# Bias rows by copies on GpSimd, index weights turned through DRAM, and two small sample blocks moved behind the value bundles

## The chip, the core and the metric

The kernel runs on one core of one Trainium2 chip. The metric is device time in microseconds (us) of one launch, and the profile is one execution of the same program.

## What is computed

One step of a hybrid layer for two requests that share every weight: a prompt of 256 frames and a sample of 32 new frames of a running stream (T = 288 rows of width 1024 together). One input projection gives everything. Branch A is an mLSTM (4 heads of 256, gates, state). Branch B is sparse attention (8 heads of 128). In it an indexer with 8 heads of 64 scores the keys,

```
score[t, s] = sum_h w[t, h] * relu(q_idx[t, h] . k_idx[s])     # w scaled by constants
keep the 64 best (prompt) or 72 best (sample) keys of a row
logits = q . k * 128**-0.5 + rel_bias[bucket(s - t)]           # 32 buckets, 8 heads
```

and the kept keys are attended to. Both branches go through gates and output weights, then a residual and a layer norm. All of it is float32; products of large size are made in two parts (a high and a low part of each operand, three matmuls).

## The kernel before

**Tiles and slots.** The weights are cut into 117 tiles of 128x1024, in the order of `ORDER`: the small columns (`sm`: index key, gates, index weights), index queries, `qb`/`kb` of branch B, its values `vb`, then `qa`/`ka`/`va`, gates, and the output weights. One tile is one slot. In each slot the tile is multiplied with x (24 matmuls of 288 columns, lines 896 to 898). In the value slots (`vb`, `va`, eight each) x stands still and the weights stream (lines 912 to 914). The sample's 32 rows are done behind every fourth value tile, in a block of 32 matmuls that each fill one strip of 32 output rows (line 920). I call this block the value bundle's strip block.

**What sets the order.** It is written out: `side()` runs in the middle of each slot's matmuls. It first runs jobs set for that slot by `at`, then one step of each generator in `procs`; a `yield` ends a step. Engines keep program order. Weight tiles come by `load_tile` on SyncE's queue (line 121), nine slots ahead, into 8 buffers. ScalarE makes the high part (line 132), VectorE the low part (line 139). A value tile's buffer is free only when the strip block has read it.

**The bias table** (`bias_table`, from slot 8). A one-hot matrix of 576 columns and the 32x8 `rel_bias` give an 8x576 table by four matmuls in slot 9, copied to SBUF by ScalarE. Two slots on SyncE writes rows of it to DRAM (line 218) and reads them back shifted as the bias `bm` and `bms`.

**The index weights** (`index_weights`, started in slot 7). They are rows 68 to 75 of the small tile `sm`. Three transposes on the matrix engine (lines 279, 280) turn them; VectorE scales them into `wn` and `wp0` and copies `ws` together (lines 282 to 288). `index()` uses them from slot 8 on, the sample's `ws` in slot 11.

**The sample's logits** (`attn_sample`, line 496) are 32 matmuls into strips of 32 rows, in the slot in which `bm` has been masked, four slots behind the last `vb` tile. VectorE and ScalarE then do the softmax (lines 502 to 506). **The sample's mLSTM scores** (`mlstm_sample`, line 718) are 16 recorded matmuls of 32x32 in slot `zb` 2, behind the transposes of attention head 7 (line 568).

**Banks.** Matmul results lie in two banks for the slots' products (`proj`) and six for all else (`bank`); a value bundle holds three of the six.

Of the kernel before, what the change touches and what calls it, by code (L numbers as in the profile page):

```python
# [10 lines left out]
F32 = mybir.dt.float32  # L11
# [23 lines left out]
ALPHA = 2.0 ** 0.25  # L35
LN_EPS = 1e-5
HEAD_EPS = 1e-6
NREL = 576
REL0 = 287
MASK = -1e30  # L40
NOT_ADMISSIBLE = -3.0e38
TAKEN = -3.39e38
# [43 lines left out]
def body(ctx, tc, a, o):  # L86
# [10 lines left out]
    def bank(name, n=512):  # L97
        return ps.tile([128, 512], F32, name=name, tag="side", bufs=6)
# [56 lines left out]
    bms = early[:, 512:1088].rearrange("p (g t) -> p g t", g=2)  # L155
    kiT = early[:, 1088:1376]
    cki = early[:, 1376:1632]
    early2 = sb("early2", [128, 2 * NREL], tag="vaT")
    oneh = early2[:32, 0:NREL]
    rtab = early2[:8, NREL:2 * NREL]  # L160
    lead = [sb(f"wst_k{k}", [128, KT * 128], tag="wst", bufs=8) for k in range(KT)]
    cut = T + 128
    sp.dma_start(lead[0][:, 0:cut], a["first"][:, 0, 0:cut])
# [21 lines left out]
    sp.dma_start(cst, a["cst"])  # L185
    load_tile(FIRST + 3)
    ident, smask, stack = cst[:, 0:128], cst[:, 128:160], cst[:, 160:288]
    relb = sb("relb", [32, 8])
    sp.dma_start(relb, a["rel_bias"])
    sp.dma_start(oneh, a["onehot"])  # L190
    load_tile(FIRST + 4)
    for c in range(2):
        sp.dma_start(cki[64 * c:64 * c + 64], a["cache_idx_k"])
# [3 lines left out]
    def bias_table():  # L197
        r = rtab
        row = dr.tile([8, 384], F32, name="rrow")
        rows = dr.tile([8, 320], F32, name="rrows")  # L200
        scr = dr.tile([128, 8, 384], F32, name="rscr")
        scs = dr.tile([TS, 8, 320], F32, name="rscs")
        early3 = sb("early3", [128, NREL + 256], F32R, tag="a5")
        onehr, rel = early3[:, :NREL], early3[:, NREL:]
        relh, rell = rel[:, 0:128], rel[:, 128:256]
        pool.memset(early3.bitcast(F32), 0.0)
        act.copy(onehr[:32], oneh)
        act.copy(relh[:32, :8], relb)
        dve.tensor_tensor(rell[:32, :8], relb, relh[:32, :8].bitcast(F32), OP.subtract)
        yield  # L210
        half = NREL // 2
        for c in (0, half):
            p = bank(f"rb{c}")
            pe.matmul(p[:, :half], lhsT=relh, rhs=onehr[:, c:c + half], start=True, stop=False)
            pe.matmul(p[:, :half], lhsT=rell, rhs=onehr[:, c:c + half], start=False, stop=True)
            act.copy(r[:, c:c + half], p[:8, :half])
        yield
        sp.dma_start(row, r[:, REL0 - 255:REL0 + 129])
        sp.dma_start(rows, r[:, 0:320])
        yield  # L220
        yield
        for c in range(0, 128, 64):
            sp.dma_start(scr[c:c + 64], ap_of(row, 0, [[0, 64], [1, 8 * 384]]))
            yield
        sp.dma_start(scs, ap_of(rows, 0, [[0, TS], [1, 8 * 320]]))
        yield
        yield
        yield
        bm = sb("bm", [128, 8, 384], tag="a5")
        store["bm"] = bm  # L230
        sp.dma_start(bm[:, :, 0:256], ap_of(scr, 127, [[8 * 384 - 1, 128], [384, 8], [1, 256]]))
        yield
        for i in range(4):
            sp.dma_start(bms[32 * i:32 * i + 32],
                         ap_of(scs, i * 320 + 31, [[8 * 320 - 1, TS], [4 * 320, 2], [1, T]]))
        yield
        yield
        pool.tensor_copy(bm[:, :, 256:384], bm[:, :, 128:256])
# [1 line left out]
    start(8, bias_table())  # L240


    wn = sb("wn", [128, 2, 8])
    wp0 = sb("wp0", [128, 4])
    ws = sb("ws", [128, 2])
    gnat = sb("gnat", [128, 2, 3, 4])
# [12 lines left out]
    def small_parts():  # L259
        sm = store["sm"]  # L260
        act.copy(kiT[0:64], sm[0:64])
        dve.tensor_copy(kiT[64:128], sm[0:64])
        act.copy(kih, kiT[:, :TP])
        dve.tensor_tensor(kil, kiT[:, :TP], kih.bitcast(F32), OP.subtract)
        gt = sb("gt", [4, 7, T], tag="stC")
        ig, z = gt[:, 0], gt[:, 1]
        store["gt"] = gt
        store["ig"], store["z"] = ig, z
        act.activation(ig, sm[64:68], AF.Identity, bias=small[:, 0:1])
        dve.tensor_scalar(z, sm[96:100], small[:, 1:2], None, op0=OP.add)  # L270
        start(cur[0] + 1, gates())
        start(cur[0] + 1, index_weights())
        at(cur[0] + 3, lambda: sp.dma_start(o["idx_k"], kiT[0:64]))

    def index_weights():
        sm = store["sm"]
        p = bank("wn_p")
        for b in range(2):
            pe.transpose(p[:, 128 * b:128 * b + 128], sm[:, 128 * b:128 * b + 128], ident)
        pe.transpose(p[:TS, 256:384], sm[:, TP:T], ident)  # L280
        c8 = float(np.float32(IH ** -0.5))
        dve.tensor_scalar(wn[:, 0], p[:, 128 + 68:128 + 76], c8, ID ** -0.5, op0=OP.mult, op1=OP.mult)
        dve.tensor_scalar(wn[:TS, 1], p[:TS, 256 + 68:256 + 76], c8, ID ** -0.5, op0=OP.mult, op1=OP.mult)
        for e in range(2):
            dve.tensor_scalar(wp0[64 * e:64 * e + 64], p[64:128, 68 + e:76:2], c8, ID ** -0.5, op0=OP.mult, op1=OP.mult)
        yield
        for i in range(4):
            dve.tensor_copy(ws[32 * i:32 * i + 32], wn[:TS, 1, 2 * i:2 * i + 2])

    def gates():  # L290
        ig, z = store["ig"], store["z"]
# [96 lines left out]
    def index():  # L388
# [3 lines left out]
        for j in range(IH // 2):  # L392
# [8 lines left out]
            for e in range(2):  # L401
                h = 2 * j + e
                n = 256 + 128 * e
                r = sb(f"r{h}", [128, 384], tag="lg", bufs=3)
                act.activation(r[:, :n], p[e][:, :n], AF.Relu)
                for c, w in ((slice(0, 256), wn[:, 0, h:h + 1]), (slice(256, 384), wp0[:, j:j + 1]))[:1 + e]:
                    if j == 0 and (e == 0 or c.start):
                        dve.tensor_scalar(acc[:, c], r[:, c], w, None, op0=OP.mult)
                    else:
                        dve.scalar_tensor_tensor(acc[:, c], r[:, c], w, acc[:, c], op0=OP.mult, op1=OP.add)  # L410
# [73 lines left out]
        pe.matmul(out, lhsT=lh, rhs=rl, start=False, stop=False)  # L484
        pe.matmul(out, lhsT=ll, rhs=rh, start=False, stop=last)

    def attn_sample():
        while "masked" not in store:
            yield
        two = range(2)  # L490
        q = [bank(f"as{g}") for g in two]
        for c, keys in ((slice(0, 256), lazy["ckT"]), (slice(256, T), kbT[:, :, TP:T])):
            for g in two:
                for i in range(4):
                    h = 4 * g + i
                    pe.matmul(q[g][32 * i:32 * i + 32, c], lhsT=qbT[:, h, TP:T], rhs=keys[:, h], start=True, stop=True)
        lgs = []
        for g in two:
            lg = sb(f"lgs{g}", [128, 384], tag="lg", bufs=3)[:, :T]
# [190 lines left out]
    def head_norm(h, num, emn, **kw):  # L690
# [18 lines left out]
            act.activation(hn[:, b], num[b][:, 0:256], AF.Identity, bias=dd[:, b, 0:1], scale=dd[:, b, 1:2])  # L709
        return hn  # L710

    def mlstm_sample():
        stC = lazy["stC"]
        q3 = qaT[:, :, TP:T]
        s = bank("ss")
        for h in range(AH):
            for kd in range(2):
                pe.matmul(s[32 * h:32 * h + 32, 0:TS], lhsT=kaT[:, 2 * h + kd, TP:T], rhs=q3[:, 2 * h + kd],
                          start=(kd == 0), stop=(kd == 1))
        tail = sb("tail", [128, 2, 4, TS], tag="ba", bufs=2)  # L720
        for kd in range(2):
            pool.tensor_copy(tail[:, kd], kaT[:, kd:8:2, TP:T])
# [178 lines left out]
    def values(t, n, k, side):  # L901
        if k == 0:
            b = [bank(f"{n}p{i}") for i in range(3)]
            lazy["vp"] = b[:2] + [out_bank(t) for _ in range(2)] + b[2:]
        banks = lazy["vp"]
        wh, wl = split.pop(t)
        for i in range(4):
            if i == 2:
                side()
            r = slice(128 * (i // 2), 128 * (i // 2) + 128)  # L910
            c = slice(512 * (i % 2), 512 * (i % 2) + 512)
            pe.matmul(banks[i], lhsT=xh[:, k, r], rhs=wh[:, c], start=(k == 0), stop=False)  # L912
            pe.matmul(banks[i], lhsT=xh[:, k, r], rhs=wl[:, c], start=False, stop=False)  # L913
            pe.matmul(banks[i], lhsT=xl[:, k, r], rhs=wh[:, c], start=False, stop=(k == KT - 1))  # L914
        if k % 4 == 3:
            for kk in range(k - 3, k + 1):
                g = 2 if n == "vb" else 1
                w = stage[t - k + kk].rearrange("p (g i c) -> p i g c", g=g, i=4)
                for i in range(4):
                    pe.matmul(banks[4][32 * i:32 * i + 32, 0:256].rearrange("p (g c) -> p g c", g=g),  # L920
                              lhsT=xs0[:, kk], rhs=w[:, i], start=(kk == 0), stop=(kk == KT - 1))
        return banks if k == KT - 1 else None

    def natural(t, rows, columns=(0, 1)):
        k = t - POS["wo", 0]
# [176 lines left out]
def constants():  # L1102
# [3 lines left out]
    s, l = np.meshgrid(i, i, indexing="ij")  # L1106
    cst[:, 128:160] = np.tile(np.where(s > l, MASK, 0.0)[:TS, :TS], (4, 1))
    cst[:, 160:288] = i[:, None] % 32 == i[None, :] % 32
    rel = np.arange(NREL) - REL0
    n = np.abs(rel)  # L1110
    bucket = np.where(n < 8, n, 8 + sum((n >= c).astype(np.int64) for c in (12, 16, 23, 32, 46, 64, 91)))
    bucket = bucket + np.where(rel > 0, 16, 0)
    onehot = np.zeros((32, NREL), np.float32)
    onehot[bucket, np.arange(NREL)] = 1.0
    return cst, onehot


def pack_weights(x, w_in, w_out_a, w_out_b, w_o):
# [76 lines left out]
```

## Time and profile before

| | |
|---|---|
| time, median of 3 runs | 428.74 us (428.34 to 429.11) |
| profiled execution, own time | 429.2 us |
| its span, first to last instruction | 427.1 us |
| granted TensorE clock | 0.999 of full speed |
| PE (matmul) busy | 420.4 us, 98% |
| VectorE (DVE) busy | 299.0 us, 70% |
| ScalarE (ACT) busy | 226.7 us, 53% |
| GpSimd (POOL) busy | 22.6 us, 5% |

Busy time counts an instruction from its start to its end; matmuls overlap, so a matmul of 0.29 us may start 0.13 us behind the one before. What a stretch costs is read from starts. In a timeline a row is start, duration, engine, line, operation, output <- inputs, shape and count (several of one kind are merged), and in brackets the idle time of its engine before it and what ended that. SPq rows are the issue of DMAs, not the transfers.

### The profile page before, as it was taken

The numbers are of one execution on the slowest core, as the hardware profiler recorded it, in microseconds if no ns is written. First come the engines' busy times: TensorE is split into PE (matmuls) and PEld (weight loads), VectorE is DVE, ScalarE is ACT, GpSimd is POOL, SyncE is SP. The second block draws the span as 40 slices with busy tenths as digits, with TensorE's granted clock in tenths as the row PEclk, the third lists the DMA queues.
The fourth block names the chain that finished last, engine by engine and source line by source line (L and its number), as shares of the span: only waits on it lengthen the run. The fifth ranks groups of instructions, "written<-read, shape, count | busy, mean of one in ns | idle before, by whom it ended". The sixth has DMA issues, their size and how long they took to land.

```text
span 427.1 us, 8153 instructions
## 1 busy us (share of the span) xinstructions
PE 420.4 (98%) x3189; PEld 395.6 (93%) x3189; DVE 299.0 (70%) x601; ACT 226.7 (53%) x443; POOL 22.6 (5%) x41
## 2 busy tenths in 40 slices
PE   8999999999999999999999999999999999999994
PEld 7999999878999998789999999999999999998874
DVE  5669989986756665665999987876454465665674
ACT  6776445425666666458795465555434444446402
POOL 0000000000400000000001101101000000000031
PEclk9999999999999999999999999999999999999999
DMA  8987869575945630349544456545555658543014
GB/s 305 362 319 206 294 204 309 214 198 204 411 156 147 218 122 0 114 141 335 152 148 150 109 171 215 148 148 151 168 178 155 176 163 265 153 137 124 27 46 140
DMA packets 29746, 78.81 MB, mean 185 GB/s; under 512 B 8548, under 2 KB 11852, under 8 KB 28908
## 3 DMA queue, kind: packets, MB, share of 16 engines
q1 hardware_dynamic: 28844, 76.98, 56.0%
q10 hardware_dynamic: 864, 1.32, 0.9%
q8 instruction: 25, 0.41, 0.4%
q14 instruction: 13, 0.11, 0.1%
HBM read 72.52 MB, written 7.67 MB: 188 GB/s over the span
## 4 chain that ended last, share of the span: by engine, by line
PE 96%; DVE 1%; ACT 1%; POOLq 0%; issue 0%; DVEq 0%; ACTq 0%
PE pj L896 22%; PE pj L897 22%; PE pj L898 21%; PE yn L938 5%; PE pj L957 3%; PE pj L912 2%; PE pj L914 2%; PE pj L913 2%; PE warm_p L150 1%; PE vap L912 1%; PE vbp L912 1%; PE vbp L914 1%; PE vap L920 1%; PE vbp L920 1%; PE vap L914 1%; PE vbp L913 1%
## 5 line engine op out<-in xcount | busy, mean ns | idle before, releaser
L132 ACT CAST wh<-wst 128x1024 fp32r<-128x1024 f32 x112 | 117.8, 1052 | 137.5 <-PE pj L897 64.8
L896 PE MATMUL pj<-xh,wh 128*128 128x288 f32 x576 | 171.7, 298 | 0.1
L897 PE MATMUL pj<-xl,wh 128*128 128x288 f32 x576 | 169.9, 295 | 0.0
L898 PE MATMUL pj<-xh,wl 128*128 128x288 f32 x576 | 169.8, 295 | 0.0
L139 DVE TENSOR_TENSOR wl<-wst,wh 128x1024 fp32r<-128x1024 f32 x112 | 136.3, 1219 | 32.2 <-ACT wh L132 31.9
L896 PEld LDWEIGHTS pj<-xh,wh 128*128 128x128 f32 x576 | 108.3, 188 | 1.8 <-issue 0.4
L897 PEld LDWEIGHTS pj<-xl,wh 128*128 128x128 f32 x576 | 108.3, 188 | 0.1
L898 PEld LDWEIGHTS pj<-xh,wl 128*128 128x128 f32 x576 | 108.3, 188 | 0.0
L896 PE MATMUL pj<-bbh,wh 128*128 128x288 f32 x64 | 18.9, 295 | 0.0
L897 PE MATMUL pj<-bal,wh 128*128 128x288 f32 x64 | 18.9, 295 | 0.0
L898 PE MATMUL pj<-bah,wl 128*128 128x288 f32 x64 | 18.9, 295 | 0.0
L897 PE MATMUL pj<-bbl,wh 128*128 128x288 f32 x64 | 18.9, 295 | 0.0
L898 PE MATMUL pj<-bbh,wl 128*128 128x288 f32 x64 | 18.8, 294 | 0.0
L896 PE MATMUL pj<-bah,wh 128*128 128x288 f32 x64 | 18.8, 293 | 0.0
L912 PE MATMUL pj<-wh,xh 128*128 128x512 f32 x32 | 13.0, 405 | 0.0
L938 PE MATMUL yn<-wh,mxh 128*128 128x512 f32 x32 | 12.9, 404 | 0.0
L938 PE MATMUL yn<-wl,mxh 128*128 128x512 f32 x32 | 12.7, 397 | 0.1
L913 PE MATMUL pj<-wl,xh 128*128 128x512 f32 x32 | 12.6, 394 | 0.0
L914 PE MATMUL pj<-wh,xl 128*128 128x512 f32 x32 | 12.6, 394 | 0.0
L938 PE MATMUL yn<-wh,mxl 128*128 128x512 f32 x32 | 12.6, 394 | 0.0
L896 PEld LDWEIGHTS pj<-bbh,wh 128*128 128x128 f32 x64 | 12.1, 188 | 0.0
L896 PEld LDWEIGHTS pj<-bah,wh 128*128 128x128 f32 x64 | 12.0, 188 | 0.0
(490 smaller groups left out, 672.2 us busy)
## 6 DMA issues: line engine op xcount, KB each, us to landing
wst<-in_w SPq DMA_DIRECT2D x112, 512.0 KB, 4.0
wst_k<-in_first SPq DMA_DIRECT2D x7, 464.0 KB, 5.0
rscr<-rrow SPq DMA_DIRECT2D x2, 768.0 KB
out_k<-kbT SPq DMA_DIRECT2D x1, 1152.0 KB
stC<-in_state_C SPq DMA_DIRECT2D x1, 1028.0 KB, 5.9
out_C_sample<-stC SPq DMA_DIRECT2D x1, 1028.0 KB
bm<-rscr SPq DMA_DIRECT2D x1, 1024.0 KB
ckT<-in_cache_k SPq DMA_DIRECT2D x1, 1024.0 KB
```

The costliest lines, as they stand in the source:

```text
L132: act.copy(split[t][0], stage[t])
L139: dve.tensor_tensor(wl, stage[t], wh.bitcast(F32), OP.subtract)
L150: pe.matmul(wp[:, :256], lhsT=warm[:, :128], rhs=warm, start=True, stop=True)
L896: pe.matmul(p[:, :T], lhsT=wh[:, c], rhs=h[:, k], start=(k == 0), stop=False)
L897: pe.matmul(p[:, :T], lhsT=wh[:, c], rhs=l[:, k], start=False, stop=False)
L898: pe.matmul(p[:, :T], lhsT=wl[:, c], rhs=h[:, k], start=False, stop=(k == KT - 1))
L912: pe.matmul(banks[i], lhsT=xh[:, k, r], rhs=wh[:, c], start=(k == 0), stop=False)
L913: pe.matmul(banks[i], lhsT=xh[:, k, r], rhs=wl[:, c], start=False, stop=False)
L914: pe.matmul(banks[i], lhsT=xl[:, k, r], rhs=wh[:, c], start=False, stop=(k == KT - 1))
L920: pe.matmul(banks[4][32 * i:32 * i + 32, 0:256].rearrange("p (g c) -> p g c", g=g), lhsT=xs0[:, kk], rhs=w[:, i], start=(kk == 0), stop=(k ...
L938: pe.matmul(p, lhsT=x[:, k, r], rhs=w[:, c], start=first and i == 0, stop=last and i == 2)
L957: pe.matmul(p[t][:, new], lhsT=w[:, 128 * t:128 * t + 128], rhs=x[:, k, new], start=(k == 0 and w is wh and x is xh), stop=(k == KT - 1 an ...
```

## The change

Three things are changed.

- The one-hot matrix and its four matmuls are left out. `rel_bias` comes from the host transposed (8 rows, 32 columns, then the first 8 reversed), and GpSimd writes the table of 416 columns by 18 copies: two plain ones and 16 that repeat one column over a run.
- The index weights are not transposed on the matrix engine. SyncE writes their 8 rows to DRAM in slot 6, reads them back turned in slot 7 (`wn` and two halves of `wp0`), and in slot 8 as `ws` (four pieces). VectorE scales them behind that, in slots 8 and 9.
- The matmuls of the sample's logits and of its mLSTM scores stand in functions of their own, called at the end of the last `vb` and the last `va` tile, straight behind the strip block.

```diff
     def bias_table():
-        pool.memset(early3.bitcast(F32), 0.0)
-        act.copy(onehr[:32], oneh)
-        act.copy(relh[:32, :8], relb)
-        dve.tensor_tensor(rell[:32, :8], relb, relh[:32, :8].bitcast(F32), OP.subtract)
-        yield
-        half = NREL // 2
-        for c in (0, half):
-            p = bank(f"rb{c}")
-            pe.matmul(p[:, :half], lhsT=relh, rhs=onehr[:, c:c + half], start=True, stop=False)
-            pe.matmul(p[:, :half], lhsT=rell, rhs=onehr[:, c:c + half], start=False, stop=True)
-            act.copy(r[:, c:c + half], p[:8, :half])
+        pool.tensor_copy(r[:, REL0 - 7:REL0 + 1], rbt[:, 32:40])
+        pool.tensor_copy(r[:, REL0 + 1:REL0 + 8], rbt[:, 17:24])
+        for i, n in enumerate(RUNS):
+            end = RUNS[i + 1] if i < 7 else 288
+            pool.tensor_copy(r[:, REL0 - end + 1:REL0 - n + 1], rbt[:, 8 + i:9 + i].to_broadcast([8, end - n]))
+            end = min(end, 129)
+            pool.tensor_copy(r[:, REL0 + n:REL0 + end], rbt[:, 24 + i:25 + i].to_broadcast([8, end - n]))
+            if i == 3:
+                yield
         yield
         sp.dma_start(row, r[:, REL0 - 255:REL0 + 129])
...
-        start(cur[0] + 1, index_weights())
+        procs.append(index_weights())
...
     def index_weights():
-        p = bank("wn_p")
-        for b in range(2):
-            pe.transpose(p[:, 128 * b:128 * b + 128], sm[:, 128 * b:128 * b + 128], ident)
-        pe.transpose(p[:TS, 256:384], sm[:, TP:T], ident)
+        rows = dr.tile([8, T], F32, name="rwi")
+        sp.dma_start(rows, store["sm"][68:76])
+        yield
+        sp.dma_start(wn, ap_of(rows, 128, [[1, 128], [T, 8], [1, 1]]))
+        for e in range(2):
+            sp.dma_start(wp0[64 * e:64 * e + 64], ap_of(rows, e * T + 64, [[1, 64], [2 * T, 4], [1, 1]]))
+        yield
+        for i in range(4):
+            sp.dma_start(ws[32 * i:32 * i + 32], ap_of(rows, 2 * i * T + TP, [[1, TS], [T, 2], [1, 1]]))
...
+        for w in (wn, wp0):
+            dve.tensor_scalar(w, w, c8, ID ** -0.5, op0=OP.mult, op1=OP.mult)
+        yield
+        dve.tensor_scalar(ws, ws, c8, ID ** -0.5, op0=OP.mult, op1=OP.mult)
...
+    def sample_logits():
+        lazy["as"] = q = [bank(f"as{g}") for g in two]
...
+    def sample_scores():
+        lazy["ss"] = s = bank("ss")
...
     def values(t, n, k, side):
-        return banks if k == KT - 1 else None
+        if k < KT - 1:
+            return None
+        if n == "vb":
+            sample_logits()
+        else:
+            sample_scores()
+        return banks
```

## Rows read from the trace of the kernel before

**Rows 1.** The chain that ended last: shares of the span by engine.

```profile
PE 96%; DVE 1%; ACT 1%; POOLq 0%; issue 0%; DVEq 0%; ACTq 0%
```

**Rows 2.** Timeline of PE around the index weights' transposes (columns: section above).

```profile
27.60 0.30 PE L898 MATMUL pj<-xh,wl 128*128 128x288 f32 x1
...
28.20 0.30 PE L897 MATMUL pj<-xl,wh 128*128 128x288 f32 x1
```

**Rows 3.** Timeline of PE around the bias table's products.

```profile
34.98 0.29 PE L898 MATMUL pj<-xh,wl 128*128 128x288 f32 x1
...
35.95 0.29 PE L897 MATMUL pj<-xl,wh 128*128 128x288 f32 x1
36.08 0.30 PE L898 MATMUL pj<-xh,wl 128*128 128x288 f32 x1
```

**Rows 4.** Timeline of PE around the sample's logits.

```profile
113.19 0.29 PE L898 MATMUL pj<-xh,wl 128*128 128x288 f32 x1
113.42 1.07 PE L496 MATMUL as<-ckT,qbT 128*32 128x256 f32 x16
...
114.78 0.29 PE L897 MATMUL pj<-xl,wh 128*128 128x288 f32 x1
```

**Rows 5.** Timeline of PE at the end of the last branch B value tile.

```profile
100.24 1.93 PE L920 MATMUL vbp<-wst,xs 128*32 128x256 f32 x32
...
102.34 0.29 PE L897 MATMUL pj<-xl,wh 128*128 128x288 f32 x1
```

**Rows 6.** Timeline of PE around transposes without and with the mLSTM scores.

```profile
195.34 0.49 PE L568 MATMUL apt<-cst,lg 128*128 128x128 f32 x3
...
195.80 0.29 PE L897 MATMUL pj<-xl,wh 128*128 128x288 f32 x1
...
202.60 0.49 PE L568 MATMUL apt<-cst,lg 128*128 128x128 f32 x3
203.02 0.35 PE L718 MATMUL ss<-qaT,kaT 128*32 128x32 f32 x16
...
203.54 0.30 PE L897 MATMUL pj<-xl,wh 128*128 128x288 f32 x1
```

**Rows 7.** Timeline of PE at the start of the second slot behind the logits.

```profile
119.27 0.29 PE L898 MATMUL pj<-xh,wl 128*128 128x288 f32 x1
...
119.89 0.29 PE L897 MATMUL pj<-xl,wh 128*128 128x288 f32 x1
```

**Rows 8.** Timeline of ACT there.

```profile
119.20 0.40 ACT L830 ACTIVATE kaT<-pj 128x288 f32<-128x288 f32 x1
```

**Rows 9.** Timeline of DVE from the masking to the sample's softmax.

```profile
107.54 1.23 DVE L139 TENSOR_TENSOR wl<-wst,wh 128x1024 fp32r<-128x1024 f32 x1 [4.01 <-ACT wh L132]
...
114.62 0.46 DVE L502 SCALAR_TENSOR_TENSOR lgs<-as,early 128x288 f32<-128x288 f32 x1 [1.07 <-PE as L496]
```

**Rows 10.** Timeline of DVE in the first index slot.

```profile
33.26 1.23 DVE L139 TENSOR_TENSOR wl<-wst,wh 128x1024 fp32r<-128x1024 f32 x1
...
36.24 1.22 DVE L139 TENSOR_TENSOR wl<-wst,wh 128x1024 fp32r<-128x1024 f32 x1
```

**Rows 11.** Timeline of PE, first matmul that reads that second low part.

```profile
41.55 0.29 PE L898 MATMUL pj<-xh,wl 128*128 128x288 f32 x1
```

**Rows 12.** Timeline of SyncE's DMA issues: weight loads, bias rows, gate columns.

```profile
20.91 2.18 SPq L121 DMA_DIRECT2D wst<-in_w  x2
...
38.62 0.50 SPq L218 DMA_DIRECT2D rrow<-early  x1
...
92.64 3.89 SPq L351 DMA_DIRECT2D gns<-rgate  x3
```

**Rows 13.** DMA issues: count, KB each, median us from issue to landing.

```profile
early<-in_cache_idx_k SPq DMA_DIRECT2D x2, 64.0 KB, 5.1
...
early<-rscs SPq DMA_DIRECT2D x4, 72.0 KB, 6.8
```

**Rows 14.** Groups of POOL by shape: busy us, mean ns of one | idle before.

```profile
L1030 POOL COPY nr<-mv 32x1 f32<-32x1 f32 x4 | 0.8, 194 | 0.2
```

More of the change, by code (lines that the diff above doesn't have):

```diff
@@ L37 @@
 HEAD_EPS = 1e-6
-NREL = 576
+NREL = 416
 REL0 = 287
+RUNS = (8, 12, 16, 23, 32, 46, 64, 91)
 MASK = -1e30
@@ L157, in body @@
     cki = early[:, 1376:1632]
-    early2 = sb("early2", [128, 2 * NREL], tag="vaT")
-    oneh = early2[:32, 0:NREL]
-    rtab = early2[:8, NREL:2 * NREL]
+    early2 = sb("early2", [8, NREL + 40], tag="vaT")
+    rtab, rbt = early2[:, 0:NREL], early2[:, NREL:]
     lead = [sb(f"wst_k{k}", [128, KT * 128], tag="wst", bufs=8) for k in range(KT)]
@@ L187, in body @@
     ident, smask, stack = cst[:, 0:128], cst[:, 128:160], cst[:, 160:288]
-    relb = sb("relb", [32, 8])
-    sp.dma_start(relb, a["rel_bias"])
-    sp.dma_start(oneh, a["onehot"])
+    sp.dma_start(rbt, a["rel_bias"])
     load_tile(FIRST + 4)
@@ L202, in bias_table @@
         scs = dr.tile([TS, 8, 320], F32, name="rscs")
-        early3 = sb("early3", [128, NREL + 256], F32R, tag="a5")
-        onehr, rel = early3[:, :NREL], early3[:, NREL:]
-        relh, rell = rel[:, 0:128], rel[:, 128:256]
-        pool.memset(early3.bitcast(F32), 0.0)
-        act.copy(onehr[:32], oneh)
-        act.copy(relh[:32, :8], relb)
-        dve.tensor_tensor(rell[:32, :8], relb, relh[:32, :8].bitcast(F32), OP.subtract)
-        yield
-        half = NREL // 2
-        for c in (0, half):
-            p = bank(f"rb{c}")
-            pe.matmul(p[:, :half], lhsT=relh, rhs=onehr[:, c:c + half], start=True, stop=False)
-            pe.matmul(p[:, :half], lhsT=rell, rhs=onehr[:, c:c + half], start=False, stop=True)
-            act.copy(r[:, c:c + half], p[:8, :half])
+        pool.tensor_copy(r[:, REL0 - 7:REL0 + 1], rbt[:, 32:40])
[7 more added lines that the diff above has]
+                yield
         yield
@@ L240, in body @@
     start(8, bias_table())
-    wn = sb("wn", [128, 2, 8])
+    wn = sb("wn", [128, 8])
     wp0 = sb("wp0", [128, 4])
@@ L271, in small_parts @@
         start(cur[0] + 1, gates())
-        start(cur[0] + 1, index_weights())
+        procs.append(index_weights())
         at(cur[0] + 3, lambda: sp.dma_start(o["idx_k"], kiT[0:64]))
     def index_weights():
-        sm = store["sm"]
-        p = bank("wn_p")
-        for b in range(2):
-            pe.transpose(p[:, 128 * b:128 * b + 128], sm[:, 128 * b:128 * b + 128], ident)
-        pe.transpose(p[:TS, 256:384], sm[:, TP:T], ident)
-        c8 = float(np.float32(IH ** -0.5))
-        dve.tensor_scalar(wn[:, 0], p[:, 128 + 68:128 + 76], c8, ID ** -0.5, op0=OP.mult, op1=OP.mult)
-        dve.tensor_scalar(wn[:TS, 1], p[:TS, 256 + 68:256 + 76], c8, ID ** -0.5, op0=OP.mult, op1=OP.mult)
+        rows = dr.tile([8, T], F32, name="rwi")
+        sp.dma_start(rows, store["sm"][68:76])
+        yield
+        sp.dma_start(wn, ap_of(rows, 128, [[1, 128], [T, 8], [1, 1]]))
         for e in range(2):
-            dve.tensor_scalar(wp0[64 * e:64 * e + 64], p[64:128, 68 + e:76:2], c8, ID ** -0.5, op0=OP.mult, op1=OP.mult)
+            sp.dma_start(wp0[64 * e:64 * e + 64], ap_of(rows, e * T + 64, [[1, 64], [2 * T, 4], [1, 1]]))
         yield
         for i in range(4):
-            dve.tensor_copy(ws[32 * i:32 * i + 32], wn[:TS, 1, 2 * i:2 * i + 2])
+            sp.dma_start(ws[32 * i:32 * i + 32], ap_of(rows, 2 * i * T + TP, [[1, TS], [T, 2], [1, 1]]))
+        c8 = float(np.float32(IH ** -0.5))
+        for w in (wn, wp0):
+            dve.tensor_scalar(w, w, c8, ID ** -0.5, op0=OP.mult, op1=OP.mult)
+        yield
+        dve.tensor_scalar(ws, ws, c8, ID ** -0.5, op0=OP.mult, op1=OP.mult)
     def gates():
@@ L405, in index @@
                 act.activation(r[:, :n], p[e][:, :n], AF.Relu)
-                for c, w in ((slice(0, 256), wn[:, 0, h:h + 1]), (slice(256, 384), wp0[:, j:j + 1]))[:1 + e]:
+                for c, w in ((slice(0, 256), wn[:, h:h + 1]), (slice(256, 384), wp0[:, j:j + 1]))[:1 + e]:
                     if j == 0 and (e == 0 or c.start):
@@ L485, in three @@
         pe.matmul(out, lhsT=ll, rhs=rh, start=False, stop=last)
-    def attn_sample():
-        while "masked" not in store:
-            yield
+    def sample_logits():
         two = range(2)
-        q = [bank(f"as{g}") for g in two]
+        lazy["as"] = q = [bank(f"as{g}") for g in two]
         for c, keys in ((slice(0, 256), lazy["ckT"]), (slice(256, T), kbT[:, :, TP:T])):
@@ L496, in attn_sample @@
                     pe.matmul(q[g][32 * i:32 * i + 32, c], lhsT=qbT[:, h, TP:T], rhs=keys[:, h], start=True, stop=True)
+    def attn_sample():
+        while "masked" not in store:
+            yield
+        two = range(2)
+        q = lazy["as"]
         lgs = []
@@ L710, in head_norm @@
         return hn
+    def sample_scores():
+        lazy["ss"] = s = bank("ss")
+        for h in range(AH):
+            for kd in range(2):
+                pe.matmul(s[32 * h:32 * h + 32, 0:TS], lhsT=kaT[:, 2 * h + kd, TP:T], rhs=qaT[:, 2 * h + kd, TP:T],
+                          start=(kd == 0), stop=(kd == 1))
     def mlstm_sample():
@@ L714, in mlstm_sample @@
         q3 = qaT[:, :, TP:T]
[L715 to L719, printed above, removed]
+        s = lazy["ss"]
         tail = sb("tail", [128, 2, 4, TS], tag="ba", bufs=2)
@@ L1108, in constants @@
     cst[:, 160:288] = i[:, None] % 32 == i[None, :] % 32
[L1109 to L1115, printed above, removed]
+    return cst
 def pack_weights(x, w_in, w_out_a, w_out_b, w_o):
@@ L1151 @@
     x = np.concatenate([f(x_prompt)[0], f(x_sample)[0]], axis=0)
-    cst, onehot = constants()
+    cst = constants()
+    rb = f(rel_bias).T
     st = np.concatenate([f(state_C)[0], f(state_n)[0][:, :, None]], axis=2)
@@ L1159 @@
         "cst": cst,
-        "onehot": onehot,
         "small": c(np.stack([f(b_gates)[:4], f(b_gates)[4:], f(state_m)[0]], axis=1)),
-        "rel_bias": f(rel_bias),
+        "rel_bias": c(np.concatenate([rb, rb[:, 7::-1]], axis=1)),
         "a_norm_g": c(f(a_norm_g).reshape(8, 128).T),
```

## The prediction

> **What bounds the kernel now.** I read the chain of waits first: grouped by engine, it lies on the matrix engine (PE) for 96% of the span [rows 1]. A kernel like that gets faster by what is taken off PE, and by the places where PE itself stands. So the second view is PE's timeline around each instruction that the change touches, where I read start to start and not durations, since matmuls overlap. The plain stream has a start every 0.13 us (35.95 to 36.08 [rows 3]); whatever a block adds to that step is what it costs. The third view is the timelines of VectorE (DVE), ScalarE (ACT), GpSimd (POOL) and SyncE's DMA issues (SP), to see whether the work that leaves PE comes back as a wait.
>
> **The change part by part.** The sum is made against the profiled execution (429.2 us, span 427.1); the median of the runs shown is 428.74, 0.46 lower, and I take the same saving off it.
>
> *Weights' transposes.* Three transposes stand between the matmuls that start at 27.60 and 28.20 [rows 2]. Plain steps would take 2 x 0.13, so they cost 0.60 - 0.26 = 0.34 us of PE. They go.
>
> *Bias table's products.* Four matmuls stand between 34.98 and 35.95 [rows 3]: 0.97 - 0.26 = 0.71 us. They go, with ACT's and DVE's casts and evictions for them, which are not on the chain.
>
> *Sample's logits* (32 matmuls into 32-row strips). Where they are, the stream goes from 113.19 to 114.78 [rows 4]: 1.59 - 0.26 = 1.33 us. From their own first start to that last one they take 114.78 - 113.42 = 1.36. In the new place they follow 32 matmuls of the same strip form (same 128x256 on 128x32). Those take 1.93 for eight groups of four [rows 5], and the logits' 16 of that shape 1.07 for four groups [rows 4], so a group costs (1.93 - 1.07) / 4 = 0.215 and the last group of the value bundle begins at 100.24 + 7 x 0.215 = 101.75. Today the stream reaches its second plain matmul 102.34 - 101.75 = 0.59 later; with the logits it will be 0.215 + 1.36 = 1.575 later. Added there: 0.99. Net gain 1.33 - 0.99 = 0.34: the way into and out of the strip form is paid once instead of twice. Bounds: 0 if the logits cost as much behind the bundles as alone, about 0.4 if the first group also starts at once.
>
> *Sample's mLSTM scores.* Now: transposes at 202.60, scores at 203.02, second plain matmul at 203.54, 0.94 in all. The same transposes without scores take 195.80 - 195.34 = 0.46 [rows 6]. So they cost 0.48. Behind the other value bundle (same form as rows 5; there are two such ends) they add 0.215 + (203.54 - 203.02) - 0.59 = 0.15. Net 0.33; bounds 0 and 0.48.
>
> The sum on PE: 0.34 + 0.71 + 0.34 + 0.33 = 1.72 us.
>
> *A stall that goes with the logits.* From 119.27 to 119.89 PE makes two steps in 0.62 instead of 0.26: it stood 0.36 [rows 7]. What it waited for ends in ACT's kaT eviction, 119.20 + 0.40 [rows 8], which stands behind the sample's softmax on ACT. That softmax starts on DVE at 114.62 after DVE had idled 1.07 for the logits [rows 9]. With the logits done some 11 us earlier that idle goes, and DVE can start at 113.55. DVE's work before it runs on from 107.54, where a 4.01 wait for the split of a weight tile ended. This tile's buffer is freed by the value bundle's strip matmuls (100.24, [rows 5]), which come 0.34 + 0.71 = 1.05 earlier and ahead of the logits. So I take it that this chain moves with them: kaT ends at 119.60 - 1.07 - 1.05 = 117.48, and PE asks at 119.40 - 1.05 - 0.34 = 118.01. No stall: 0.36 more. If only the idle goes and the DMA behind 107.54 does not move, kaT ends at 118.53 and PE waits 118.53 - 118.01 = 0.52 for it, against 119.60 - 119.40 = 0.20 now: the change loses 0.32 here. Late next is ACT's split of the next tile, on the same chain.
>
> *POOL's copies.* 18 copies of 8 partitions. Nearest row: 32x1 copies at 194 ns [rows 14], so 18 x 0.19 = 3.5 us on an engine with nothing else to do then. Their reader is the row DMA at 38.62 [rows 12]. Even if they began only at 31.3 (the table's first slot, halfway between the slots of 27.60 and 34.98) they could take 7.3 / 18 = 0.41 each before SP had to wait. Cost taken: 0. If the cover were gone, SP would issue weight loads later, and those have slots in hand.
>
> *The weights' round trip.* SP now also issues one write, three loads behind a wait for it, and four more a slot later; all pass through SP's one queue. The write goes out behind the load that ends at 20.91 + 2.18 = 23.1 [rows 12]. Small transfers among the weight loads land after 5.1 (median of the two nearest), at most 6.8 in this listing [rows 13]. Issuing three took 3.89 us where the queue was full of element transfers [rows 12]; as a low value I use 0.5 each, as for the bias row at 38.62. So: 23.1 + 0.5 + 5.1 = 28.7 for the write, + 1.5 + 5.1 = 35.3 for the loads; late bound 23.1 + 0.5 + 6.8 + 3.9 + 6.8 = 41.1. I take 35.3, since those transfers stand beside the same loads. SP's weight loads behind this wait go out up to some us late and are used many slots later. On DVE the scaling waits, and behind it stand the index sums and the split of the tile that PE needs at 41.55 [rows 11]. DVE reaches it at 33.26 + 1.23 = 34.49 and from there to the end of that split takes 36.24 + 1.22 - 34.49 = 2.97 [rows 10]. PE will ask at 41.55 - 1.05 = 40.50, so landings up to 40.50 - 2.97 = 37.5 cost nothing. 35.3 is inside, by 2.2 us. The four small loads are read a slot later with more room. The removed copies (DVE and ACT) are a gain on engines off the chain: 0.
>
> The Trainium skill's page "DMA: Bandwidth & Descriptors" (Rules for kernel authors) speaks against this part: a plain DMA with a rearranged access pattern is the slow way to transpose, and a strided last dimension becomes one descriptor per element. By that rule the landing moves toward the late bound, which is the first rival below. The trace has such transfers for the gates, and the 3.89 us for issuing three is what they show of it [rows 12].
>
> Total: 1.72 + 0.36 = 2.08, so 428.74 - 2.08 = 426.66, say 426.7 us.
>
> **The rivals.**
>
> *The round trip is late (slower).* Place: DVE's scaling of the weights in the first index slot. Price: each us of landing after 37.5 is a us of PE, standing for the split tile. For: three transfers in a row, each behind loads, and SP's 3.89 for three. Against: 2.2 us in hand at nearest rows, and 1,792 elements in all where one gate load alone has 1,536. At the late bound 41.1 it costs 3.6: 428.74 - 2.08 + 3.6 = 430.3. From 39.6 on it eats the whole gain. Chance 0.07.
>
> *The sample's softmax keeps PE waiting.* ACT and DVE don't move with PE at 107 to 119 (their wait at 107.54 is for a load, [rows 9]): 1.72 - 0.32 = 1.40, so 427.3. Against: the buffer of that load is freed by PE. Chance 0.18.
>
> *The merge does not do what it says.* The matmuls behind the bundles pay the change of form anyway, or wait there for a bank: net 0 for logits and scores, leaving 1.05, with or without the 0.36: 427.3 to 427.7. For: the bundles hold three of the six side banks. Against: the logits' inputs are long there, and groups of one form follow at 0.215 inside a block. Chance 0.10. Together with the kept stall it is 1.05 - 0.32 = 0.73: 428.0, no change that can be told; chance 0.05.
>
> **How the numbers follow.** The forecast has 0.60. The measurement can't tell less than 0.2% (0.86 us) from no change, so "faster" begins below 427.9. Faster: 0.60 + 0.18 + 0.10 less 0.06 for smaller sizes = 0.82. Same: 0.05 + 0.06 and 0.02 of the late round trip = 0.13. Slower: the rest of that rival, 0.05. Range: the forecast's own error is some 0.8 either way (bounds of the merged blocks, stall, the median's own 0.4), 425.9 below; above, it takes in both middle rivals and ends at 428.2.
>
> **What would show it.** Right: no PE work between the plain matmuls of the slots at 27 and 34; behind both value bundles a single strip block with no gap above 0.22 inside, 0.99 and 0.15 longer; DVE's first softmax step with no idle for PE; no PE stall at kaT. Wrong: a DVE idle on a DMA at 34 to 37 that ends after 37.5 with PE standing in front of the next tile; PE standing at 118; the first strip group of logits or scores as late as after a plain matmul.

## The result and the profile after

The changed kernel takes 426.03 us (median of 6 runs, 425.87 to 426.87) against 428.65 of the kernel before (6 runs): ratio 0.9944, 95% interval 0.9933 to 0.9956. It is 2.62 us faster, where 2.08 was forecast. Two launches, one of the changed kernel (1457 us) and one of a variant below (1593 us), were disturbed and are left out everywhere. The profiled execution took 425.94 us with a span of 424.2. Line numbers differ in the kernel after: weight products are L897 to L899, the strip block L921, logits L488, scores L714, DVE's split L140, ACT's L133. The variants below have numbers of their own.

The page's first part for the changed kernel (busy us, share of the span, instructions) shows that PE lost 2.7 us of busy time (420.4 before) and 7 matmul records (3189 before), and POOL has 17 instructions more (41 before; 18 copies for a memset).

```profile
PE 417.7 (98%) x3182; PEld 394.3 (93%) x3182; DVE 298.6 (70%) x595; ACT 225.4 (53%) x439; POOL 24.1 (6%) x58
```

Timeline of PE, changed kernel (start us, us, engine, line, operation, out<-in, count). Read start to start.

```profile
4.87 0.40 PE L964 MATMUL pj<-xh,wh_k 128*128 128x288 f32 x1
...
27.25 0.29 PE L897 MATMUL pj<-xh,wh 128*128 128x288 f32 x1
27.38 0.29 PE L898 MATMUL pj<-xl,wh 128*128 128x288 f32 x1
...
34.29 0.29 PE L897 MATMUL pj<-xh,wh 128*128 128x288 f32 x1
34.42 0.29 PE L898 MATMUL pj<-xl,wh 128*128 128x288 f32 x1
...
98.71 1.93 PE L921 MATMUL vbp<-wst,xs 128*32 128x256 f32 x32
100.46 1.05 PE L488 MATMUL as<-ckT,qbT 128*32 128x256 f32 x16
101.33 0.31 PE L488 MATMUL as<-kbT,qbT 128*32 128x32 f32 x16
101.56 0.40 PE L897 MATMUL pj<-xh,wh 128*128 128x288 f32 x1
101.80 0.29 PE L898 MATMUL pj<-xl,wh 128*128 128x288 f32 x1
...
117.27 0.30 PE L898 MATMUL pj<-xl,wh 128*128 128x288 f32 x1
117.40 0.29 PE L899 MATMUL pj<-xh,wl 128*128 128x288 f32 x1
117.53 0.29 PE L897 MATMUL pj<-xh,wh 128*128 128x288 f32 x1
...
189.50 1.93 PE L921 MATMUL vap<-wst,xs 128*32 128x256 f32 x32
191.25 0.34 PE L714 MATMUL ss<-qaT,kaT 128*32 128x32 f32 x16
...
191.77 0.29 PE L898 MATMUL pj<-xl,wh 128*128 128x288 f32 x1
...
200.48 0.49 PE L566 MATMUL apt<-cst,lg 128*128 128x128 f32 x3
...
200.94 0.30 PE L898 MATMUL pj<-xl,wh 128*128 128x288 f32 x1
```

At 27.25 and 34.29 plain steps of 0.13 stand where the transposes [rows 2] and the table's products [rows 3] were. The value block with the logits goes from 98.71 to the second plain matmul at 101.80: 3.09, against 2.10 without them [rows 5], so they add 0.99. The other block takes 191.77 - 189.50 = 2.27, so the scores add 0.17; the transposes alone now take 0.46 (200.48 to 200.94) instead of 0.94 [rows 6]. At 117.40 there is no stall [rows 7].

Timelines of the other engines in the changed kernel: first DVE (idle before an instruction and what ended it in brackets).

```profile
33.30 0.17 DVE L280 TENSOR_SCALAR wn<-wn 128x8 f32<-128x8 f32 x1
33.37 0.16 DVE L280 TENSOR_SCALAR wp<-wp 128x4 f32<-128x4 f32 x1
...
34.64 1.22 DVE L140 TENSOR_TENSOR wl<-wst,wh 128x1024 fp32r<-128x1024 f32 x1
36.99 0.17 DVE L282 TENSOR_SCALAR ws<-ws 128x2 f32<-128x2 f32 x1 [1.13 <-DMA ws<-rwi]
...
105.99 1.23 DVE L140 TENSOR_TENSOR wl<-wst,wh 128x1024 fp32r<-128x1024 f32 x1 [4.00 <-ACT wh L133]
...
112.06 0.46 DVE L500 SCALAR_TENSOR_TENSOR lgs<-as,early 128x288 f32<-128x288 f32 x1
```

Then ACT, SP's queue and POOL.

```profile
113.35 0.52 ACT L502 ACTIVATE lgs<-lgs,sts 128x288 f32<-128x288 f32 x1
...
116.93 0.40 ACT L831 ACTIVATE kaT<-pj 128x288 f32<-128x288 f32 x1
```

```profile
22.70 0.30 SPq L270 DMA_DIRECT2D rwi<-early  x1
...
28.24 0.38 SPq L272 DMA_DIRECT2D wn<-rwi  x1
28.67 2.57 SPq L274 DMA_DIRECT2D wp<-rwi  x2
...
37.02 0.50 SPq L211 DMA_DIRECT2D rrow<-early  x1
```

```profile
18.32 0.18 POOL L201 COPY early<-early 8x8 f32<-8x8 f32 x1 [17.81 <-DMA early<-in_rel_bias]
...
20.39 0.34 POOL L205 COPY early<-early 8x197 f32<-8x197 f32 x1
20.68 0.20 POOL L207 COPY early<-early 8x38 f32<-8x38 f32 x1
```

The sample's softmax starts on DVE without idle time [rows 9], kaT is there at 117.33 [rows 8], the scaling of `wn` and `wp0` waits for no DMA, and POOL is done 16 us before the row DMA at 37.02 reads the table [rows 12]. The scaling of `ws`, a slot later, does wait: 1.13 us for its load, until 36.99. PE makes plain steps there, so it costs nothing.

### The profile page after: what moved, and what is told of

It reads as the page before. It is cut to its first block, busy times and chain, and to the rows that moved or that the text cites. A ratio compares the mean times of both kernels' runs of the same rounds, so it can differ in the third digit from the quotient of the medians.

```text
span 424.2 us, 8152 instructions
## 1 busy us (share of the span) xinstructions
PE 417.7 (98%) x3182; PEld 394.3 (93%) x3182; DVE 298.6 (70%) x595; ACT 225.4 (53%) x439; POOL 24.1 (6%) x58
## 3 DMA queue, kind: packets, MB, share of 16 engines
q10 hardware_dynamic: 864, 1.32, 0.9%
## 4 chain that ended last, share of the span: by engine, by line
PE 96%; DVE 1%; DMA 1%; POOLq 0%; ACT 0%; DVEq 0%; issue 0%
PE pj L898 22%; PE pj L897 22%; PE pj L899 22%; PE yn L945 5%; PE pj L964 3%; PE pj L915 2%; PE pj L914 2%; PE pj L913 2%; PE vap L913 1%; PE vbp L913 1%; PE vbp L915 1%; PE vap L921 1%; PE vbp L921 1%; PE vap L914 1%; PE vbp L914 1%; PE vap L915 1%
## 5 line engine op out<-in xcount | busy, mean ns | idle before, releaser
L133 ACT CAST wh<-wst 128x1024 fp32r<-128x1024 f32 x112 | 117.8, 1052 | 140.5 <-PE pj L898 67.8
L897 PE MATMUL pj<-xh,wh 128*128 128x288 f32 x576 | 171.3, 297 | 0.0
L899 PE MATMUL pj<-xh,wl 128*128 128x288 f32 x576 | 169.7, 295 | 0.0
L140 DVE TENSOR_TENSOR wl<-wst,wh 128x1024 fp32r<-128x1024 f32 x112 | 136.3, 1219 | 31.4 <-ACT wh L133 31.0
L897 PEld LDWEIGHTS pj<-xh,wh 128*128 128x128 f32 x576 | 108.3, 188 | 0.6 <-issue 0.4
L899 PEld LDWEIGHTS pj<-xh,wl 128*128 128x128 f32 x576 | 108.2, 188 | 0.0
L899 PE MATMUL pj<-bah,wl 128*128 128x288 f32 x64 | 18.9, 296 | 0.0
L897 PE MATMUL pj<-bbh,wh 128*128 128x288 f32 x64 | 18.9, 295 | 0.0
L897 PE MATMUL pj<-bah,wh 128*128 128x288 f32 x64 | 18.8, 294 | 0.0
L899 PE MATMUL pj<-bbh,wl 128*128 128x288 f32 x64 | 18.8, 294 | 0.0
L897 PEld LDWEIGHTS pj<-bbh,wh 128*128 128x128 f32 x64 | 12.0, 188 | 0.0
L898 PEld LDWEIGHTS pj<-bbl,wh 128*128 128x128 f32 x64 | 12.0, 188 | 0.0
```

The source lines that it names most:

```text
L133: act.copy(split[t][0], stage[t])
L140: dve.tensor_tensor(wl, stage[t], wh.bitcast(F32), OP.subtract)
L897: pe.matmul(p[:, :T], lhsT=wh[:, c], rhs=h[:, k], start=(k == 0), stop=False)
L898: pe.matmul(p[:, :T], lhsT=wh[:, c], rhs=l[:, k], start=False, stop=False)
L899: pe.matmul(p[:, :T], lhsT=wl[:, c], rhs=h[:, k], start=False, stop=(k == KT - 1))
```

## The experiments

The additive theory says that each term of the sum stands by itself. Its rivals: the merge saves nothing of its own; the gain beyond the sum comes from the start, where the memset on POOL is gone (rival S); the round trip has a point from which it costs. Times are medians, ratios stand against the kernel before on the same chip.

**Both moves taken back** (table and weights as changed; the calls stand in `attn_sample` and `mlstm_sample` again):

```diff
+        sample_logits()
...
+        sample_scores()
...
-        if n == "vb":
-            sample_logits()
-        else:
-            sample_scores()
-        return banks
+        return banks if k == KT - 1 else None
```

> The changed kernel with both moves taken back: the sample's logits and the mLSTM scores are issued by their own procedures again, between plain matmuls; the bias copies and the weights' round trip stay. Additive theory (each PE term stands by itself): only the transposes' 0.34 and the table's 0.71 are left, 428.65 - 1.05 = 427.6 us, 1.57 slower than the changed kernel's 426.03; the gap of some 0.36 in front of the products behind the logits, which waits for kaT, is back. Rival S (the missing POOL memset lets the first DMA land earlier and gives 0.5 more): 427.1 us. Rival 'the moves save nothing of their own': 426.0 us.

Measured: 427.35 us, ratio 0.9968 (0.9956 to 0.9981). The stall is back, on PE's timeline of this kernel:

```profile
118.49 0.29 PE L901 MATMUL pj<-xh,wl 128*128 128x288 f32 x1
118.86 0.40 PE L899 MATMUL pj<-xh,wh 128*128 128x288 f32 x1
```

and DVE waits for the logits again:

```profile
113.84 0.46 DVE L501 SCALAR_TENSOR_TENSOR lgs<-as,early 128x288 f32<-128x288 f32 x1 [2.05 <-PE as L488]
```

A step of 0.37 instead of 0.13. The time lies between the additive 427.6 and S's 427.1; where the missing 0.25 went is told below (*What the sum had not*). Over the stretch of the last table below, this kernel is 1.08 faster than before (1.05 worked out) and 0.96 slower than the changed one, so the moves do save something of their own. Against before, the starts of equal matmuls shift by 0.33 at the transposes and by 0.71 at the table's products, each by itself.

**The moves alone**, in the kernel before (with the two functions):

```diff
+        if n == "vb":
+            sample_logits()
+        else:
+            sample_scores()
```

> The kernel before with the two moves alone: table still made by products and evacuations, weights still turned by four transposes, POOL's memset of the start still there. Additive theory: logits 0.34, stall 0.36, scores 0.33 = 1.03, so 428.65 - 1.03 = 427.6 us; at the merge PE steps some 0.98 more behind the value bundles and 1.33 less where the logits stood. Rival S agrees in the time, and has the first product start at 5.07 us as before, not at 4.87. Rival 'the moves save nothing of their own': 428.65 us.

Measured: 427.69 us, ratio 0.9978 (0.9969 to 0.9987): 1.00 us faster, 1.03 expected. PE's steps are the expected ones: by the starts of equal matmuls, 0.99 more behind the value bundle, 1.32 less where the logits stood, 0.36 less at the stall, and for the scores 0.16 more and 0.48 less. (The kernel before has three transposes, not four as the expectation says.) Both halves add up in the last table, 1.08 + 0.98 = 2.06 against 2.04 to 2.07; in the medians they make 1.34 + 1.00 = 2.34, less than the 2.62 of the first comparison.

**The logits early, but apart from the strip block:**

```diff
-        if n == "vb":
-            sample_logits()
-        else:
+        if n == "va":
             sample_scores()
...
+    at(POS["qa", 0], sample_logits)
```

> The changed kernel with the logits issued early, but apart from the strip block of the value bundles: between the plain matmuls of the next slot (qa0). Additive theory: the strip form is entered and left once more, so the logits cost the 1.33 that they cost in the kernel before and not 0.98; the stall for kaT stays gone because the masked softmax still starts early: 426.03 + 0.35 = 426.4 us. Rival W (the whole gain of the move comes from the wait that goes, not from the two strip blocks lying together): 426.0 us.

Measured: 426.50 us, ratio 0.9952 (0.9939 to 0.9964). PE's timeline of this kernel around the logits:

```profile
102.11 0.29 PE L899 MATMUL pj<-xh,wl 128*128 128x288 f32 x1
102.34 1.07 PE L488 MATMUL as<-ckT,qbT 128*32 128x256 f32 x16
103.23 0.31 PE L488 MATMUL as<-kbT,qbT 128*32 128x32 f32 x16
103.46 0.40 PE L897 MATMUL pj<-xh,wh 128*128 128x288 f32 x1
103.70 0.29 PE L898 MATMUL pj<-xl,wh 128*128 128x288 f32 x1
```

The stream goes from 102.11 to its second plain matmul behind them at 103.70: 1.59 - 0.26 = 1.33, as in the kernel before [rows 4], where behind the block they add only 0.99. Both edges are seen: 0.23 into the block instead of 0.13, and 0.24 from the first plain matmul behind it to the second (103.46 to 103.70). No stall appears at kaT. So the logits' move has two separate gains: about 0.34 from lying beside a block of its form, and 0.36 from an earlier softmax. That the wait alone explains it (W) falls. The scores were not set apart in this way: their gain is measured, but that it comes from the form is argued from the logits.

**The POOL memset kept at the start:**

```diff
+        early3 = sb("early3", [128, 832], F32R, tag="a5")
+        pool.memset(early3.bitcast(F32), 0.0)
```

> The changed kernel with a POOL memset of 128x832 put back at the start (its tile is read by nobody). Additive theory, which takes the 0.49 at the start and the 0.36 at the end for differences between launches: 426.0 us. Rival S (the memset delays the first DMA's landing): 426.5 us, with the first product at 5.07 and the first products at 0.61 each, as in the kernel before.

Measured: 426.24 us, ratio 0.9947 (0.9935 to 0.9960). No 0.5 us. The first cast began at 4.52 us, against 4.59 and 4.38 in the profiles before and after, which left a smaller effect open. So the other side was tried.

**The memset held back in the kernel before:**

```diff
+        pool.tensor_copy(r[:, 0:8], relb[:8])
         pool.memset(early3.bitcast(F32), 0.0)
```

> The kernel before with POOL's memset held back: a copy of 8x8 that waits for the relative bias (some 18 us) stands ahead of it on POOL. Rival S in its smaller size (the memset costs the first transfer's landing 0.2 us): ScalarE's first cast at 4.3 to 4.4 us instead of 4.59, 428.65 - 0.2 = 428.45 us. If the landings of 4.59, 4.63 and 4.52 with the memset against 4.38, 4.38 and 4.30 without it were chance: 4.59 and 428.65.

Measured: 428.65 us in ten runs, ratio 0.9996 (0.9987 to 1.0005): no difference in time, although the first cast came at 4.21.

**The changed kernel again**, twice, without an edit:

> The changed kernel once more, for the part of its gain that the path does not explain. Additive theory with 0.2 for the memset: 428.65 - 2.06 - 0.2 = 426.4 us, first cast at 4.3 to 4.4 us, the rise of TensorE's clock at a moment that differs from launch to launch (it was 4.1 in the first profile of this kernel, 6.0 in that of the kernel before, 7.0 in that without the moves), so the profiled span up to 0.3 us longer than the 424.2 of the first profile. If the clock's rise belongs to the change: at 4.1 us again, 426.0 us.

> The changed kernel once more. Launches of one kernel differ by the moment at which TensorE's step halves (4.1 to 7.0 us in the profiles so far), worth up to 0.75 us: 426.2 us, between 425.8 and 427.0 for a single time, with TensorE's steps at the two merged blocks and the two slots without the products as in the first profile (within 0.02).

Measured: 426.15 to 427.00 us in four runs, ratio 0.9942 (0.9928 to 0.9955), and 426.24 us with ratio 0.9952 (0.9937 to 0.9967). Only the second has a profile to read. In it the first cast is at 4.55 us, among the values with the memset. As a cause of time S falls, in both sizes: the memset put back cost nothing that can be told (426.24), and holding it back gained nothing (428.65). Whether the first cast itself comes a little later with it stays open: 4.52 to 4.63 in three profiles with the memset at the start, 4.21 to 4.55 in nine without. The second theory held: PE's steps are those of the first profile, and the span is 0.6 longer by the start alone. The first product in the kernel without the moves shows how much a launch can differ there:

```profile
4.86 0.61 PE L960 MATMUL pj<-xh,wh_k 128*128 128x288 f32 x1
```

In the changed kernel's first profile the same product starts at 4.87 but takes 0.40.

**The round trip made longer**, by n more copies of the rows in DRAM (n = 1, 2, 3, 5):

```diff
+        more = [dr.tile([8, T], F32, name=f"rwi{i}") for i in range(n)]
+        for nxt in more:
+            sp.dma_start(nxt, rows)
+            rows = nxt
```

> The changed kernel with one more copy of the index weights' rows in DRAM (8x288, read by the same loads), so that wn, wp0 and ws land later by one transfer. Rival 'the round trip is late', with its point at 37.5 us: VectorE's scaling waits until some 37 to 38.5 us and its split of the next weight tile behind it; 0 to 1 us slower than the changed kernel, 426.0 to 427.0. If VectorE's wait is hidden whatever its length: 426.0 us.

> The same with two more copies. Rival 'the round trip is late': the scaling waits until some 41 to 43 us, 4 to 5 us past its point of 37.5, and TensorE stands for about as long in front of a product that needs the split weight tile: 429.5 to 431 us. If VectorE's wait is hidden whatever its length: 426.0 us.

Measured: 426.28 us, ratio 0.9937 (0.9923 to 0.9950), and 426.69 us, ratio 0.9944 (0.9932 to 0.9957): no loss that can be told, with two copies too. The second expectation was a miss: the second copy put the last scaling off by 2.2 us (35.60 to 37.80), not by 4 to 5. DVE's timeline with two copies:

```profile
36.92 0.17 DVE L284 TENSOR_SCALAR wn<-wn 128x8 f32<-128x8 f32 x1 [2.78 <-DMA wn<-rwi]
37.80 0.17 DVE L284 TENSOR_SCALAR wp<-wp 128x4 f32<-128x4 f32 x1 [0.71 <-DMA wp<-rwi]
...
38.98 1.22 DVE L140 TENSOR_TENSOR wl<-wst,wh 128x1024 fp32r<-128x1024 f32 x1
```

The split ends at 40.20, and PE loads its tile at 40.64: still hidden, by 0.44. This launch was some 0.8 late from its start on. Three and five copies go past the point:

> The changed kernel with three more copies of the index weights' rows in DRAM. With none, one and two the last scaling began at 33.37, 35.60 and 37.80 us: 2.2 us for each. With two the split behind it ended at 40.20 and TensorE first used its tile at 40.64, 0.44 later, with no loss. So the point lies at 37.80 + 0.44 = 38.24 us in a launch whose first product begins some 0.07 and whose clock rises some 0.65 later than in the first profile of the changed kernel. Rival 'the round trip is late', past its point: the scaling at 40.0, TensorE stands 2.2 - 0.44 = 1.8 us in front of that tile: 426.2 + 1.8 = 428.0 us. If the slots behind win it back: 426.2.

> Five more copies. Past the point a us of landing costs a us of TensorE: the scaling at 44.4, TensorE stands 6.6 - 0.44 = 6.2 us: 426.2 + 6.2 = 432.4 us, slower than the kernel before. If SyncE's queue, which holds the weight loads behind the wait, starves the next tiles as well: more than that.

Measured: 428.07 us, ratio 0.9989 (0.9980 to 0.9998), and 433.97 us, ratio 1.0118 (1.0103 to 1.0133). With three, DVE and then PE:

```profile
38.67 0.17 DVE L284 TENSOR_SCALAR wp<-wp 128x4 f32<-128x4 f32 x1 [0.48 <-DMA wp<-rwi]
...
39.82 1.22 DVE L140 TENSOR_TENSOR wl<-wst,wh 128x1024 fp32r<-128x1024 f32 x1
```

```profile
39.93 0.29 PE L902 MATMUL pj<-xl,wh 128*128 128x288 f32 x1
41.09 0.40 PE L903 MATMUL pj<-xh,wl 128*128 128x288 f32 x1 [0.87 <-DVE wl L140]
41.33 0.30 PE L901 MATMUL pj<-xh,wh 128*128 128x288 f32 x1
41.46 0.29 PE L902 MATMUL pj<-xl,wh 128*128 128x288 f32 x1
```

With five, DVE's last scaling and then PE:

```profile
43.35 0.17 DVE L284 TENSOR_SCALAR wp<-wp 128x4 f32<-128x4 f32 x1 [0.73 <-DMA wp<-rwi]
```

```profile
40.42 0.29 PE L902 MATMUL pj<-xl,wh 128*128 128x288 f32 x1
45.80 0.60 PE L903 MATMUL pj<-xh,wl 128*128 128x288 f32 x1 [5.08 <-DVE wl L140]
46.20 0.44 PE L901 MATMUL pj<-xh,wh 128*128 128x288 f32 x1
```

With three, PE would have gone on at 40.07, and from the scaling to the end of the split it is 41.04 - 38.67 = 2.37: the point lay at 40.07 - 2.37 = 37.70. It was passed by 0.97, and PE stood 41.09 - 40.07 = 1.02. The third copy put the scaling to 38.67 and not to 40.0, so PE stood less than the 1.8 expected. With five the scaling is at 43.35 and the wait 45.80 - 40.55 = 5.25; the stretch of the table below is 7.6 us longer than the changed kernel's, so more came behind the wait (last section). With three, the stretch is 1.2 longer while the median is 1.9 longer; its times go from 427.18 to 429.13, and the profiled execution was the fastest. So that the median met 428.0 is not borne out by the profile; how long PE stood in the slower launches isn't known. The rival is real: with five copies the change is a loss.

**Without the start and the end.** Start of the 21st matmul of the first products and of the last weight product, from each trace; their difference is free of what a launch does at its start.

| kernel | 21st product | last product | difference | against before | last product to span's end |
|---|---|---|---|---|---|
| before | 8.20 | 416.91 | 408.71 | | 10.22 |
| before, memset held back | 7.99 | 416.69 | 408.70 | -0.01 | 10.11 |
| changed | 7.71 | 414.38 | 406.67 | -2.04 | 9.85 |
| changed, third comparison | 8.37 | 415.01 | 406.64 | -2.07 | 9.84 |
| moves taken back | 8.47 | 416.10 | 407.63 | -1.08 | 9.90 |
| moves alone | 7.96 | 415.69 | 407.73 | -0.98 | 9.94 |
| logits apart | 7.70 | 414.69 | 406.99 | -1.72 | 9.90 |
| memset kept | 7.99 | 414.63 | 406.64 | -2.07 | 9.89 |
| one copy more | 8.43 | 415.07 | 406.64 | -2.07 | 9.91 |
| two more | 8.48 | 415.12 | 406.64 | -2.07 | 9.69 |
| three more | 7.77 | 415.60 | 407.83 | -0.88 | 9.63 |
| five more | 8.25 | 422.50 | 414.25 | +5.54 | 9.76 |

## Why the prediction was right, point by point

*The sum.* Each term came out as worked: by the shift of equal matmuls against before, the transposes give 0.33 (0.34 forecast), the table 0.71 (0.71), the logits 1.32 less 0.98 = 0.34 (0.34), the stall 0.36 (0.36), the scores 0.48 less 0.16 = 0.32 (0.33). Together 2.06, forecast 2.08, and 2.04 to 2.07 in the table.

*The stall.* The step that could have failed was "this chain moves with them": DVE's wait for the load is 4.00 as before and the split stands at 105.99 instead of 107.54, 1.55 earlier. Of that 1.05 is the forecast's and 0.49 the start of this launch. kaT ended at 117.33 (117.48 forecast), and the second rival (427.3) did not come. But the nearness of the two is luck: with the launch's 0.49 taken out, kaT came 0.34 later than forecast, since ACT, still busy with a gate matrix, took up the first logits only at 113.35, 0.35 after DVE had them ready (113.00). PE asked at 117.53, so 0.20 us was in hand, where the forecast had 118.01 - 117.48 = 0.53.

*The merge.* The third rival (the matmuls pay the change of form anyway) fell for the logits with the kernel that set them apart: 0.32 slower in the table. For the scores only the steps speak against it.

*The copies on POOL* took 2.6 us (18.32 to 20.88, 18 of them) and hid entirely, as said.

*The round trip.* The write landed where it was put: SP's first load goes out at 28.24, right behind it (28.7 forecast). The loads were faster: 33.3 at most, since the scaling did not wait, where 35.3 was forecast from 5.1 us a landing. With one copy more the scaling began 1.8 us behind the end of the last issue (33.78 to 35.60, the latter from DVE's timeline there). That term was sized too long by 2 us or more, on the safe side, and cost nothing.

The point was near: 37.5 forecast, 37.70 read off with three copies. In part that is luck: this launch ran 0.43 earlier than the profiled one of before, and behind the scaling DVE needed 2.37 us and not 2.97, so on the clock of the forecast the point lay at 38.1, again on the safe side. Its price of one us for one us held for 0.97 us past the point; with five copies more was lost than the wait.

On issuing, the three loads took 3.0 us of SP's queue (28.24 to 31.24), between the two values weighed, and their 1,536 elements had landed within 2.1 us of it. The Trainium skill's page "DMA: Bandwidth & Descriptors" (Rules for kernel authors) calls a plain DMA with a rearranged access pattern the slow way to transpose. No run here sets these loads beside another way, so how slow they are for a DMA isn't shown; in the time the rule decided nothing.

*What the sum had not.* The measured gain is 2.62 us in the first comparison. Over all runs with a span on record (47 of the kernel before, 16 of the changed one) the medians are 428.69 and 426.18, 2.51 apart. The medians of their spans are 426.6 and 424.45, 2.15 apart: inside the span the sum is met to 0.1. The other 0.36 lies outside it. Time less span is 2.00 to 2.13 us in every run of the kernel before and 2.02 to 2.09 in the moves alone, but 1.67 to 1.79 in the changed kernel, and 1.70 to 1.79 with the moves taken back or the memset put back. So this surplus goes with the new table or the turned weights, not with the moves and not with the memset; it is also the 0.25 by which the kernel without the moves beat its expectation. Which of the two it is, and why, is open. It isn't fixed either: with two more copies in DRAM it is 1.86 to 1.92, with three 1.68 to 2.05.

The end of the profiles differs too. In the table's last column stand 10.22 and 10.11 in the two kernels that hold none of the change and 9.63 to 9.94 in the ten others, 0.33 less in the mean. PE's and DVE's steps there are equal, and the last write is issued at the same distance from the last product; only its landing is later. But each entry is a single execution, and the moves alone have the short end as well (9.94) without any gain beyond the sum. So it does not explain the surplus.

No experiment points to a version that beats the changed kernel. Doing all eight value tiles of the sample in one strip block might save a way in and out once more, but would hold more weight tiles at a time; it wasn't tried.

## What to carry to other kernels

Where one engine is the whole path, price each edit by the steps from start to start of its neighbours: small blocks of another matmul form cost their way in and out, and setting them behind a block of the same form saved 0.3 us each (for the second block the reason is argued, not tested). Then read the gain inside the span before explaining what a median shows beyond the sum. When such a block moves earlier, look for a wait further down that it fed: here that was as large again. For a transfer put in place of work, compute the moment from which the engine stands, and compare that with the landing; here a landing of unknown length mattered only beyond that point.

## What the hardware showed that was not expected

TensorE's step at the start of a launch halves (0.21 to 0.11 us for the 256-column warm-up matmuls, 1.2 and 2.4 GHz) at a moment that differs from launch to launch of the same program: 4.2 us in one profile of the changed kernel, 6.8 in another (6.4 in that of the kernel before, where an expectation above says 6.0), after unbroken work from 1.1 on. In the two profiles of the changed kernel the 21st product starts at 7.71 and 8.37, 0.66 apart, of which 0.17 is the first product's own start. The profile's clock column reads 1.00 there at both steps.

After standing for 5.25 us, TensorE came back at the lower level: windows of the kernel with five copies (stretch, PE, PEld, DVE, ACT, POOL busy and count, granted clock, DMA share, GB/s).

```profile
36.00:40.00 4.00, 4.00 (x33) 4.00 (x32) 0.00 (x0) 1.73 (x3) 0.00 (x0) 1.00 0.04 5
40.00:46.00 6.00, 0.92 (x7) 0.69 (x6) 2.45 (x6) 1.72 (x3) 0.00 (x0) 0.85 0.62 104
46.00:50.00 4.00, 4.00 (x43) 3.24 (x44) 3.43 (x5) 0.00 (x0) 0.00 (x0) 0.50 0.95 277
50.00:54.00 4.00, 4.00 (x29) 4.00 (x29) 3.83 (x9) 1.35 (x2) 0.00 (x0) 0.88 0.69 179
```

The granted clock is 0.50 from 46 to 50 us and the steps are 0.24 instead of 0.13 (46.20 to 46.45). It cost 7.6 - 5.25 = 2.3 us beside the wait, and explains why this kernel is slower than the 432.4 expected. The expectation's other reason, starved tiles, is not seen: PE is busy for all of 46 to 50. The four runs agree: three had a granted clock of 0.989 or 0.990 in the mean and took 433.95 to 434.36 us; one had 0.996 and took 432.43. After standing for 1.02 us, with three copies, the steps were 0.13 again from the second matmul on (41.33 to 41.46).
